# Two x1 pieces multiplied by g_final on VectorE instead of GpSimd, with the last wide block's end sums one step later

## The chip, the cores and the metric

One core of a Trainium2 chip runs the whole kernel; the other cores are idle. The metric is device time in microseconds (us) of one execution, the median over several runs. The core has TensorE (PE in the profile, with its weight loads as PEld), VectorE (DVE), ScalarE (ACT), GpSimd (POOL) and SyncE (SP); in this kernel SP computes nothing, it issues most of the DMAs.

## The reference

One encoder layer on 256 tokens of width 4096, in float32. What matters here is its end:

```python
x = x + einsum('bse,ed->bsd', concatenate([y_a, y_b]), w_out[i])       # x1 in the kernel
ple  = einsum('bsc,cd->bsd', p[i], w_ple[i])
gate = sigmoid(einsum('bsd,de->bse', rms_norm(x, g_ple[i]), w_ple_gate[i]))
x = x + ple * gate
return rms_norm(x, g_final)          # x * rsqrt(mean(x*x) + EPS) * g_final
```

The gate is a product of 256x4096 by 4096x4096. After it every row of x is squared and summed, and multiplied by the inverse root and by g_final, a gain for each of the 4096 columns.

## The kernel before

**Products.** A float32 product is made of three matmuls (`mm`, L130): each operand is split into a high half, rounded by ScalarE (`hi`, L115), and the rest, subtracted by VectorE (`lo`, L116). Rows 0-127 and 128-255 of the tokens are t=0 and t=1. A plain step takes one slice of 128 rows of a weight matrix and runs 12 matmuls of the block's column half-width for it.

**Blocks.** A `Block` (L772) makes 1024 columns of an output (the fourth block of the gate 768, so that its matmuls are 384 wide) from 32 weight slices. Some slices are taken in pairs by Strassen's scheme: `fast_steps` (L816) turns a pair into four steps, with four subtractions of weights (`sub`, L824) and the subtraction at L839 on VectorE besides the splits. `weave` (L155) lays the steps out; for the fourth block it is six pairs with plain steps between, then a trail. When the last step of the sixth pair has run, `wide_mid` (L1022) is spawned: it copies one bank and adds four others into `e` (L1027, L1029) and sets the flag `("mid", 3)`. When the last step of the block has run, `wide_done` (L1034) adds the last four banks, the **end sums** (L1049), in one step; in the next ones it takes the tanh of a quarter (L1053, ScalarE), multiplies it with the ple product (L1055), adds it to x1 (L1057, both VectorE) and squares the result with a row sum (L1060, ScalarE), quarter after quarter; at the end it reduces the sums of squares (L1064, L1065) and sets `part2`.

**Steps after the sixth pair.** In the order of TensorE they are called here c1, c2 (plain), e1, e2 (the ple product of the block, `wide_ple`), c3, c4 (plain), small (the ple product of the last 256 columns), c5, c6 (plain; c6 is the last of the block); then the last 256 columns of the gate in steps l0 to l7, of four weight slices each. l0 to l3 run for t=0 alone, l4 to l7 for both, and four more steps run t=1 with the kept halves of l0 to l3. The plain step inside the sixth pair, between its first and second step, is called cb. `done_last` (L1094) is spawned behind l7 for t=0 and behind the last step for t=1: tanh, product, sum, squares, then `finish` (L1108), which makes the inverse root and scales the eight 512-column pieces of x1 and sends them out. Pieces 1 and 4 (`EARLY`, L986) have been multiplied by g_final before and are scaled on ScalarE (L1123); the six others take both factors at once on VectorE (L1125).

**Order.** Every engine runs its instructions in the order in which the program emits them. The loop at L1452 does this for each step: load weights ahead (`fetch`), split the weights of a step some places ahead (`convert`), run the step's matmuls, then `advance()` (L240), which gives each spawned task one turn, up to its next `yield`, in the order in which they were spawned. A step with an `after` runs and advances before it converts. Four raw weight buffers (`raw`) and a ring of three split tiles (`hi`/`lo`) limit how far ahead loads and splits go: a raw buffer is free when VectorE has subtracted from it, a split tile when TensorE has used it.

**g_final.** `load_g` (L972) is spawned at the start of the fourth block. When the fourth pair has run (`z used`) it takes the two tiles `gF` and issues, one a step, eight DMAs on SP's queue (L979), each a piece of 512 gains broadcast to 128 partitions, in the order 1, 4, 0, 2, 3, 5, 6, 7. Behind the issue of piece 1 and of piece 4 it multiplies x1 by it on GpSimd, one instruction for each t (L983), four in all. SP's queue holds the weight loads of the same steps (L800, L998) between them.

Of the kernel before, what the change touches and what calls it, by code (L numbers as in the profile page):

```python
# [15 lines left out]
ALU = mybir.AluOpType  # L16
AX = mybir.AxisListType

P = 128
S = 256  # L20
NT = S // P
# [57 lines left out]
def encoder_layer(ctx: ExitStack, tc: tile.TileContext, x, p, positions, g_mix, w_in, g_q_latent, w_uq,  # L79
                  g_kv_latent, w_ukv, g_out_mla, g_out_dil, w_out, w_ple, g_ple, w_ple_gate, g_final,  # L80
                  c_inv, c_dist, out):
    nc = tc.nc
# [11 lines left out]
    def slot(tag, shape, dtype=F32):  # L94
        names[tag] = names.get(tag, 0) + 1
        return sp.tile([P, *shape], dtype, tag=tag, name=f"{tag}_{names[tag]}")
# [137 lines left out]
    flags, urgent, waiting, running = set(), [], [], []  # L234
# [469 lines left out]
    x1 = {}  # L704
# [239 lines left out]
    FAST, WIDE = 7, 4  # L944
# [27 lines left out]
    def load_g():  # L972
        while "z used" not in flags:
            yield
        for i in range(2):
            gF.append(slot(f"B{2 + i}", [2048]))
        for c in (1, 4, 0, 2, 3, 5, 6, 7):
            g = g_cols(512 * c)
            nc.sync.dma_start(g, g_final[512 * c:512 * (c + 1)].unsqueeze(0).to_broadcast([P, 512]))  # L979
            yield  # L980
            if c in EARLY:
                for t in range(NT):
                    nc.gpsimd.tensor_tensor(x1[c][:, t], x1[c][:, t], g, op=ALU.mult)  # L983

    P4 = {}
    EARLY = 1, 4  # L986
# [47 lines left out]
    def wide_done(k, blk):  # L1034

        def pieces(h, i):
            lo, out = 1024 * k + blk.q * h, []
            while lo < 1024 * k + blk.q * (h + 1):
                n = min(512 - lo % 512, 1024 * k + blk.q * (h + 1) - lo)
                at = lo - 1024 * k - blk.q * h  # L1040
                out.append((blk.e[:, i, at:at + n], x1[lo // 512], slice(lo % 512, lo % 512 + n), 2 * k + h + len(out)))
                lo += n
            return out

        def task():
            e, ps = blk.e, blk.ps
            quarters = ((0, 0, 0, "M2"), (3, 1, 1, "X"), (1, 0, 1, "M3"), (2, 1, 0, "M4"))
            for i, t, h, m in quarters:
                nc.vector.tensor_tensor(e[:, i], e[:, i], ps[m], op=ALU.add)  # L1049
            yield  # L1050
            for n in range(6):
                for i, t, h, m in quarters[n:n + 1]:
                    nc.scalar.activation(e[:, i], e[:, i], AF.Tanh, scale=r1h[:, t:t + 1])  # L1053
                for i, t, h, m in quarters[n - 1:n] if n else ():
                    nc.vector.scalar_tensor_tensor(e[:, i], e[:, i], 1.0, P4[t, h][:, :blk.q], op0=ALU.add, op1=ALU.mult)  # L1055
                    for u, xc, at, _ in pieces(h, i):
                        nc.vector.tensor_tensor(xc[:, t, at], u, xc[:, t, at], op=ALU.add)  # L1057
                for i, t, h, m in quarters[n - 2:n - 1] if n > 1 else ():
                    for u, xc, at, c in pieces(h, i):
                        nc.scalar.activation(u, xc[:, t, at], AF.Square, accum_out=ss2[:, t, c:c + 1])  # L1060
                yield
            if k == WIDE - 1:
                for t in range(NT):
                    nc.vector.tensor_reduce(part2[t], ss2[:, t, :9], axis=AX.X, op=ALU.add)  # L1064
                    nc.vector.tensor_scalar(part2[t], part2[t], 1.0 / DM, EPS, op0=ALU.mult, op1=ALU.add)  # L1065
                flags.add("part2")
        return task
# [23 lines left out]
    def g_cols(lo):  # L1091
        return gF[lo // 2048][:, lo % 2048:lo % 2048 + 512]
# [188 lines left out]
    for k in range(WIDE):  # L1281
        q = Q if k < 3 else 384
        order = weave(*((range(6), 6, 4), (range(7), 4, 4), (range(7), 4, 4), ((1, 2, 3, 4, 0, 5), 6, 6))[k], 2)
        blk = Block(w_ple_gate[:, 1024 * k:1024 * k + 2 * q], lhs_x1, x1_s, "x1_sums", order,
                    lambda kt: [("x1T", kt // 4)], LAST, "B6", WP + ["B4"], q)
        if k == 3:
            hook(len(steps), lambda: spawn(load_g()))
        lay(blk, order, wide_mid(k, blk), wide_done(k, blk), wide_ple(k, q), **({"after": [], "used": {4: "z used"}} if k == 3 else {}))
# [225 lines left out]
```

## Time and profile before

| what | value |
|---|---|
| median of 3 runs | 1931.02 us (1930.95 to 1931.32) |
| the profiled execution | 1929.53 us, of which the span is 1927.6 us |
| TensorE busy, weight loads | 1907.9 us (99%), 1630.7 us (85%) |
| VectorE busy | 1580.6 us (82%) |
| ScalarE busy | 1112.3 us (58%) |
| GpSimd busy | 81.2 us (4%), 126 instructions |
| granted TensorE clock | 0.998 of full speed |

Busy time of TensorE is modelled from pipelined matmuls, so that a busy TensorE is not always one at its peak; the distance between the starts of matmuls says more. The median and the profiled execution differ by 1.49 us. Span times below count from the first instruction of the profiled execution; some 1.9 us of its time lie outside the span.

### The profile page before, as it was taken

How to read it: one execution, taken by the hardware profiler on the slowest of the kernel's cores; microseconds unless marked ns; L12 is line 12 of the kernel's file. 1: busy time of each engine (PE TensorE's matmuls, PEld its weight loads, DVE VectorE, ACT ScalarE, POOL GpSimd, SP SyncE). 2: the span in 40 equal slices, each digit the busy share in tenths (PEclk: the TensorE clock that was granted, in tenths of full speed). 3: DMA queues.
4: the chain of work that ended last, by engine and by line, in shares of the span. 5: the costliest groups of instructions: out<-in, count | busy, mean ns of one | idle time of the engine just before them, and what ended most of it. 6: DMA issues, size and time to landing. Idle time of an engine off the chain costs nothing.

```text
span 1927.6 us, 25662 instructions
## 1 busy us (share of the span) xinstructions
PE 1907.9 (99%) x9254; PEld 1630.7 (85%) x9254; DVE 1580.6 (82%) x2198; ACT 1112.3 (58%) x1542; POOL 81.2 (4%) x126
## 2 busy tenths in 40 slices
PE   9999999999999999999999999999999999999997
PEld 8998889998888888888888888888888888888897
DVE  7767966665999999998877778889896698989896
ACT  6555565564655555655556666555564456656654
POOL 1001011220000000000000010000000000000010
PEclk9999999999999999999999999999999999999999
DMA  7666655555666666766665456665666656565675
GB/s 252 188 187 202 192 171 146 147 146 163 188 188 204 211 214 197 211 204 193 213 194 143 132 164 221 205 216 175 224 197 217 188 186 218 187 211 193 194 218 188
DMA packets 143119, 370.58 MB, mean 192 GB/s; under 512 B 12149, under 2 KB 41681, under 8 KB 142993
## 3 DMA queue, kind: packets, MB, share of 16 engines
q1 hardware_dynamic: 141360, 363.90, 61.8%
q0 software_dynamic: 1632, 5.05, 0.7%
q8 instruction: 72, 1.18, 0.3%
q14 instruction: 55, 0.44, 0.1%
HBM read 364.72 MB, written 4.19 MB: 191 GB/s over the span
## 4 chain that ended last, share of the span: by engine, by line
PE 90%; DVE 7%; DMA 1%; ACT 1%; issue 1%; SPq 0%; DVEq 0%; ACTq 0%
PE m L134 19%; PE m L135 19%; PE m L133 19%; PE t L133 4%; PE t L135 4%; PE t L134 3%; PE s L134 3%; PE s L133 3%; PE s L135 3%; PE o L134 3%; PE o L135 3%; PE o L133 3%; DVE lo L116 2%; DVE B L824 1%; DMA raw<-in_w_ple_gate_dram 1%
## 5 line engine op out<-in xcount | busy, mean ns | idle before, releaser
L116 DVE TENSOR_TENSOR lo<-raw,hi 128x1024 fp32r<-128x1024 f32 (+4 forms) x488 | 530.7, 1093 | 210.4 <-ACT hi L115 207.9
L115 ACT ACTIVATE hi<-raw 128x1024 fp32r<-128x1024 f32 (+4 forms) x488 | 463.1, 954 | 346.5 <-PE m L135 170.2
L133 PE MATMUL m<-hi,Ah 128*128 128x512 f32 (+3 forms) x1080 | 409.9, 380 | 0.1
L134 PE MATMUL m<-lo,Ah 128*128 128x512 f32 (+3 forms) x1080 | 405.7, 376 | 3.3 <-DVE lo L116 2.1
L135 PE MATMUL m<-hi,Al 128*128 128x512 f32 (+3 forms) x1078 | 403.0, 374 | 0.0
L134 PEld LDWEIGHTS m<-lo,Ah 128*128 128x128 f32 x1080 | 203.3, 188 | 35.7 <-DVE lo L116 7.2
L135 PEld LDWEIGHTS m<-hi,Al 128*128 128x128 f32 x1078 | 202.6, 188 | 30.4 <-DVE Al L127 0.2
L133 PEld LDWEIGHTS m<-hi,Ah 128*128 128x128 f32 x1080 | 203.3, 188 | 27.8 <-ACT Ah L125 0.3
L133 PE MATMUL m<-hi,B 128*128 128x512 f32 (+1 forms) x426 | 162.5, 382 | 0.0
L134 PE MATMUL m<-lo,B 128*128 128x512 f32 (+1 forms) x426 | 158.9, 373 | 0.2 <-DVE lo L116 0.2
L135 PE MATMUL m<-hi,B 128*128 128x512 f32 (+1 forms) x426 | 158.9, 373 | 0.0
L115 ACT ACTIVATE hi<-B 128x1024 fp32r<-128x1024 f32 (+1 forms) x85 | 87.9, 1035 | 92.3 <-DVE B L824 59.9
L116 DVE TENSOR_TENSOR lo<-B,hi 128x1024 fp32r<-128x1024 f32 (+1 forms) x85 | 101.0, 1190 | 5.0 <-ACT hi L115 2.1
L824 DVE TENSOR_TENSOR B<-raw,B 128x512 f32<-128x512 f32 (+1 forms) x138 | 94.9, 687 | 0.0
L135 PEld LDWEIGHTS m<-hi,B 128*128 128x128 f32 x426 | 80.0, 188 | 11.8
L134 PEld LDWEIGHTS m<-lo,B 128*128 128x128 f32 x426 | 80.2, 188 | 11.3 <-DVE lo L116 0.9
L133 PEld LDWEIGHTS m<-hi,B 128*128 128x128 f32 x426 | 80.1, 188 | 10.5
L115 ACT ACTIVATE B<-raw 128x1024 fp32r<-128x1024 f32 (+2 forms) x68 | 61.4, 910 | 47.7 <-DMA raw<-in_w_in_dram 20.0
L115 ACT ACTIVATE B<-B 128x1024 fp32r<-128x1024 f32 (+2 forms) x62 | 59.1, 954 | 43.3 <-DVE B L824 23.7
L116 DVE TENSOR_TENSOR B<-raw,B 128x1024 fp32r<-128x1024 f32 (+2 forms) x68 | 70.2, 1039 | 13.3 <-ACT B L115 13.0
L116 DVE TENSOR_TENSOR T<-t,T 128x512 fp32r<-128x512 f32 (+1 forms) x65 | 44.4, 682 | 41.6 <-ACT T L115 41.2
L839 DVE TENSOR_TENSOR lo<-raw,hi 128x1024 fp32r<-128x1024 f32 (+1 forms) x61 | 74.3, 1218 | 2.7 <-ACT hi L837 2.7
(764 smaller groups left out, 3879.3 us busy)
## 6 DMA issues: line engine op xcount, KB each, us to landing
raw<-in_w_in_dram SPq DMA_DIRECT2D x320, 512.0 KB, 3.9
raw<-in_w_out_dram SPq DMA_DIRECT2D x128, 512.0 KB, 4.4
raw<-in_w_ple_gate_dram SPq DMA_DIRECT2D x96, 512.0 KB, 4.6
raw<-in_w_in_dram SPq DMA_DIRECT2D x63, 400.0 KB, 3.5
raw<-in_w_uq_dram SPq DMA_DIRECT2D x32, 384.0 KB, 3.4
raw<-in_w_ple_gate_dram SPq DMA_DIRECT2D x32, 384.0 KB, 3.8
raw<-in_w_ukv_dram SPq DMA_DIRECT2D x16, 512.0 KB, 4.0
raw_l<-in_w_ple_gate_dram SPq DMA_DIRECT2D x8, 512.0 KB, 4.9
```

What stands on the lines that cost most here:

```text
L115: nc.scalar.activation(hi, src, AF.Copy)
L116: nc.vector.tensor_tensor(lo, src, plain(hi), op=ALU.subtract)
L133: nc.tensor.matmul(ps, ah, bh, start=start, stop=False)
L134: nc.tensor.matmul(ps, ah, bl, start=False, stop=False)
L135: nc.tensor.matmul(ps, al, bh, start=False, stop=stop)
L824: nc.vector.tensor_tensor(dst, a, b, op=ALU.subtract)
L839: nc.vector.tensor_tensor(lo, r[1], plain(hi), op=ALU.subtract)
```

## The change

`load_g` only issues the eight loads, one a step, in the same order. Then it waits for the flag that `wide_mid` of the fourth block sets, and in the two steps after the next one multiplies piece 1, then piece 4, of x1 by g_final, two instructions each, on VectorE. Nothing is computed on GpSimd there any more. In the fourth block `wide_done` gives away one turn before its end sums, so that these and all that follows in that task come one step later.

```diff
         for c in (1, 4, 0, 2, 3, 5, 6, 7):
-            g = g_cols(512 * c)
-            nc.sync.dma_start(g, g_final[512 * c:512 * (c + 1)].unsqueeze(0).to_broadcast([P, 512]))
-            yield
-            if c in EARLY:
-                for t in range(NT):
-                    nc.gpsimd.tensor_tensor(x1[c][:, t], x1[c][:, t], g, op=ALU.mult)
+            nc.sync.dma_start(g_cols(512 * c), g_final[512 * c:512 * (c + 1)].unsqueeze(0).to_broadcast([P, 512]))
+            yield
+        while ("mid", WIDE - 1) not in flags:
+            yield
+        for c in EARLY:
+            yield
+            for t in range(NT):
+                nc.vector.tensor_tensor(x1[c][:, t], x1[c][:, t], g_cols(512 * c), op=ALU.mult)
...
             e, ps = blk.e, blk.ps
             quarters = ((0, 0, 0, "M2"), (3, 1, 1, "X"), (1, 0, 1, "M3"), (2, 1, 0, "M4"))
+            if k == WIDE - 1:
+                yield
             for i, t, h, m in quarters:
                 nc.vector.tensor_tensor(e[:, i], e[:, i], ps[m], op=ALU.add)
             yield
```

## The prediction

> **What bounds the kernel.** I read the chain of waits first, then windows around the one place where GpSimd works late in the run, then each engine's timeline there.
>
> ```profile
> PE 90%; DVE 7%; DMA 1%; ACT 1%; issue 1%; SPq 0%; DVEq 0%; ACTq 0%
> ```
>
> TensorE bounds the run, so a change is worth what it gives or takes between two matmul starts, and behind the last matmul. Three windows of 10 us (span, then busy time and count of PE, PEld, DVE, ACT, POOL; clock, DMA share, GB/s):
>
> ```profile
> 1850.00:1860.00 10.00, 9.92 (x55) 9.38 (x55) 9.71 (x16) 5.87 (x9) 0.00 (x0) 1.00 0.74 212
> 1860.00:1870.00 10.00, 8.05 (x44) 7.09 (x42) 9.30 (x9) 2.55 (x4) 6.75 (x4) 1.00 0.96 317
> 1870.00:1880.00 10.00, 9.14 (x52) 9.06 (x53) 8.23 (x11) 5.88 (x8) 0.00 (x0) 1.00 0.72 210
> ```
>
> VectorE is busy all through the middle one but runs 9 instructions where 16 ran before. Its timeline (start, duration, engine, line, operation, form), then GpSimd's:
>
> ```profile
> 1856.13 0.55 DVE L824 TENSOR_TENSOR B<-raw,B 128x384 f32<-128x384 f32 x1
> 1856.60 0.95 DVE L839 TENSOR_TENSOR lo<-raw,hi 128x768 fp32r<-128x768 f32 x1
> ...
> 1862.95 1.92 DVE L116 TENSOR_TENSOR lo<-raw,hi 128x768 fp32r<-128x768 f32 x1 [0.70 <-ACT hi L115]
> 1864.80 1.63 DVE L824 TENSOR_TENSOR B<-raw,B 128x384 f32<-128x384 f32 x1
> 1866.35 2.03 DVE L839 TENSOR_TENSOR lo<-raw,hi 128x768 fp32r<-128x768 f32 x1
> 1868.30 1.64 DVE L824 TENSOR_TENSOR B<-raw,B 128x384 f32<-128x384 f32 x1
> 1869.86 0.94 DVE L116 TENSOR_TENSOR B<-B,B 128x768 fp32r<-128x768 f32 x1
> ```
>
> ```profile
> 1862.77 6.75 POOL L983 TENSOR_TENSOR T<-T,B 128x512 f32<-128x512 f32 x4 [406.28 <-DMA B<-in_g_final_dram]
> ```
>
> The same forms take 0.95 and 0.55 us before, two to three times that while L983 runs (until 1869.52), and 0.94 again right behind it. Starts of neighbours lie some 0.08 us closer than durations, so one 768-wide subtraction occupies VectorE for 0.87 us, a 384-wide one for 0.47. The four slow ones hold it from 1862.95 to 1869.86, 6.91 us; at the usual rate 2 x 0.87 + 2 x 0.47 = 2.68. TensorE pays (its waits of more than half a microsecond from 1850 on):
>
> ```profile
> 1864.93 0.44 PE L134 MATMUL m<-lo,Ah 128*128 128x384 f32 x1 [0.58 <-DVE lo L116]
> 1868.44 0.45 PE L134 MATMUL m<-lo,Ah 128*128 128x384 f32 x1 [1.13 <-DVE lo L839]
> 1870.86 0.44 PE L134 MATMUL m<-B,B7a 128*128 128x384 f32 x1 [1.11 <-DVE B L116]
> ...
> 1897.56 0.39 PE L134 MATMUL m<-lo,Ah 128*128 128x256 f32 x1 [0.54 <-DVE lo L116]
> ```
>
> **Removed: GpSimd's four multiplications.** Matmuls of 384 columns start every 0.173 us elsewhere. cb starts at 1864.01, and 30 matmuls follow until c1: without waits c1 starts at 1864.01 + 30 x 0.1733 = 1869.21, in the trace at 1872.92. That is 3.71 us; the three idle times shown make only 2.82, since a busy record is modelled longer than the spacing and each restart costs 0.11 more. VectorE's new times meet TensorE: cb's split done at 1863.9 (needed 1864.2), L839 at 1865.3 (1866.25), the third step's split at 1866.7 (1867.3), the fourth's at 1867.6 (1868.3). **Gain 3.71.**
>
> **What is late next: c1 and e1.** The loads of c1 and c2 were issued at 1860.87 and 1862.27, before the slowdown, and took 6.6 and 6.7 us behind the g_final pieces: landed 1867.47 and 1868.97. That stays. c1: ScalarE from 1867.57 (0.10 behind the landing, as cb's split shows at 1862.07), VectorE 0.88 later for 0.95, done at 1869.40; plus 0.06 from VectorE's end to the matmul (1864.87 to 1864.93). TensorE wants it at 1869.38: 0.08 of waiting and 0.11 for the restart. c2's split starts on VectorE at 1869.98 and occupies it to 1870.85; the four sums L1029 take 2.10 (1873.55 to 1875.65 in the trace), and e1's split is done at 1870.85 + 2.10 + 0.95 = 1873.90, wanted at 1869.21 + 0.19 + 24 x 0.1733 + 0.17 = 1873.73: 0.23 + 0.11. **Loss 0.19 + 0.34 = 0.53.** With everything earlier the second ple slice (issued at 1870.00 behind L824) and g piece 7 go out at about 1865.8. In the trace the transfers of this stretch land in order of issue, at 1865.80, 1866.47, 1867.47, 1868.04, 1868.97, 1869.65, 1870.60 and 1871.17, a 384 KB load about 1 us behind the one ahead, so I let later issues delay no earlier one.
>
> **Added: four multiplications on VectorE.** 128x512 in float32 from SBUF has a row, L824 in the earlier blocks: 683 ns, some 0.60 us of VectorE's time. Piece 1 stands behind e2's split and ahead of c3's, piece 4 ahead of c4's. e2's split ends its turn at 1874.70, so c3's comes at 1875.9, is done at 1876.9 and wanted at 1878.2; c4's is done at 1878.9, wanted at 1880.3. TensorE's trail, 2.08 us a plain step against 0.87 on VectorE, hides all 4 x 0.60 = 2.4 us; without that cover it would cost 2.4. One thing is late: c4's split frees the raw buffer for l0's load, 0.9 later than if all moved by 3.2. l0's load has that much to spare (landed at 1885.5, used at 1886.35), l1's next to none, should l0 push it; l1's split frees the buffer of l5's load. Between 0 and 0.9 I take **0.2**, since l1's load, issued 1.6 behind l0's, took only 0.6 longer (4.9 against 4.3).
>
> **Moved: the end sums.** VectorE around them (same columns):
>
> ```profile
> 1894.43 1.01 DVE L1049 TENSOR_TENSOR B<-B,m 128x384 f32<-128x384 f32 x2
> ...
> 1896.29 2.35 DVE L116 TENSOR_TENSOR lo<-raw_l,hi 128x1024 fp32r<-128x1024 f32 x2
> ...
> 1904.93 1.23 DVE L116 TENSOR_TENSOR lo<-raw_l,hi 128x1024 fp32r<-128x1024 f32 x1 [0.47 <-ACT hi L115]
> ...
> ...
> 1908.34 0.42 DVE L1102 SCALAR_TENSOR_TENSOR Q<-Q,t 128x256 f32<-128x256 f32 x1 [1.66 <-ACT Q L1101]
> ```
>
> Times of this trace, as if nothing had moved: 1.86 us of sums stand ahead of l4's split; TensorE waits for that (start spacings 0.82 and 0.23 for 0.12: 0.81 lost). Behind the change l4's and l5's splits come first (VectorE 1895.07 to 1897.64), then the sums to 1899.50, l6's split to 1900.64, three quarters (L1055, L1057: 3.32 us, as 1900.00 to 1903.32) to 1903.96, and l7's split, whose high half ScalarE makes behind the second quarter's squares at 1903.64: 1904.72 to 1905.95. l4 no longer waits, but l7 does: it starts 0.2 to 0.3 sooner, not 0.8. And the fourth quarter now lies behind l7's split: its sum done at 1907.0, its square at 1907.65, the four reductions at 1908.25; only then t=0's product, 1908.3 against 1908.34. From there VectorE works without a break to the last output. **Gain 0.05**; ends: 0.8 if l7's wait also goes, a loss of 0.5 if ScalarE's squares come later than this.
>
> **Sum:** -3.71 + 0.53 + 0.2 - 0.05 = -3.0 us: span 1924.6, that execution 1926.5. The profiled execution is 1.49 under the median; the same step from the median gives 1931.02 - 3.0 = **1928.0**.
>
> **Rivals.** (1) *More comes back*: c1 and e1 don't wait, and l4's stall goes through to the end: -3.71 - 0.8 = -4.5, 1926.5; with half of the 0.53 and of the 0.8, 1927.2. For it: the margins missed are 0.1 and 0.2 us. Against it: VectorE without a break at the end. (2) *Loads move past each other*: e1's, e2's and g piece 7, now issued up to 4 us earlier, share the queue with c1 and c2 instead of following them. 640 KB at 384 KB a microsecond are 1.67; c1 0.8 and c2 1.67 later make e1's split 1.7 later than above, TensorE loses 2.2 instead of 0.53, the gain is 1.3: 1929.7. Against it stand the eight landings in order. The Trainium skill speaks for it: the page "DMA: Bandwidth & Descriptors", section "Queues, rings and completion order", says that descriptors of a queue are consumed in ring order on each engine but that completion is not first in, first out; by that rule the sum would be -1.3, by the rows -3.0. (3) *Slower*: GpSimd is not the cause. VectorE is slow from 1862.95 because the g_final transfers fill the DMA engines (share 0.96), and stays so; then nothing is gained, 2.4 us are added to VectorE, of which the trail hides most, and l0's load is late: +0.4, 1931.4, and up to 1933.4 if the 2.4 are not hidden. It decides if L824 and L839 stay over 1.5 us around 1865. Against it: VectorE ran at its usual rate from 1859.9 to 1861.7, when the transfers were already queued, and again at 1869.86, 0.3 behind GpSimd's end.
>
> **Chances.** Forecast (gain 2.2 to 3.8) 0.55; (1) beyond 3.8: 0.22; (2) 0.15; (3) 0.05; others 0.03, half of them slower by much. What a measurement of this kernel tells from no change is taken as 0.2%, 3.86 us, and the forecast lies inside: faster by more 0.23, from (1); slower by more 0.04, from the exposed end of (3) and the others; within 0.73. Range: 1926.5 is the end of (1); 1930.3 takes in (2) with 0.6 more for l1's load; outside are (3), the others and the far tails of (1) and (2), under 2 in 10.
>
> **What would show it.** Right: L839 and both L824 of the last pair near 0.95 and 0.55 us; c1 at 1869.2 to 1869.5; waits of about 0.1 and 0.2 at c1 and e1; four multiplications of 0.68 us between e2's and c4's splits with no wait of TensorE behind them; no wait at l4 but one of about half a microsecond at l7. Wrong: slow VectorE without GpSimd, landings of c1 and c2 behind 1868 and 1869.5, a wait at c3 or c4, or t=0's tanh waiting long for the last square.

## The result, and the profile after

The changed kernel takes 1926.44 us (median of 9 runs, 1924.66 to 1928.93), the kernel before 1930.95 us beside it (9 runs, 1929.42 to 1931.51). The ratio is 0.9978, 95% interval 0.9968 to 0.9988; that is 4.2 us less, between 2.3 and 6.2. The profiled execution of the changed kernel took 1926.44 us as well.

From the page of the changed kernel: its span, the busy time of each engine, and the shares of the engines in the chain of work that ended last.

```profile
span 1924.7 us, 25658 instructions
...
PE 1906.5 (99%) x9254; PEld 1630.2 (85%) x9254; DVE 1579.3 (82%) x2202; ACT 1111.8 (58%) x1542; POOL 74.4 (4%) x122
...
PE 88%; DVE 7%; DMA 2%; ACT 1%; issue 1%; SPq 0%; DVEq 0%; ACTq 0%
```

The span is 2.9 us shorter than the 1927.6 of before. Four instructions have left GpSimd (126 to 122, 6.8 us), and VectorE's busy time fell by 1.3 us although it has four more: what it got is less than what it lost. TensorE still bounds the run.

The windows around the last pair of the changed kernel (bounds, length, then busy time and count of PE, PEld, DVE, ACT, POOL; clock, DMA share, GB/s):

```profile
1860.00:1868.00 8.00, 8.00 (x48) 8.00 (x48) 6.79 (x10) 3.88 (x6) 0.00 (x0) 1.00 1.01 316
1868.00:1871.00 3.00, 3.00 (x18) 2.82 (x17) 1.95 (x3) 1.89 (x4) 0.00 (x0) 1.00 1.06 410
1871.00:1875.00 4.00, 3.84 (x23) 3.52 (x22) 3.93 (x7) 2.21 (x3) 0.00 (x0) 1.00 0.70 249
```

And the same of the kernel before:

```profile
1860.00:1868.00 8.00, 6.73 (x38) 6.09 (x36) 7.30 (x7) 2.55 (x4) 5.23 (x4) 1.00 0.97 308
1868.00:1871.00 3.00, 1.46 (x7) 1.14 (x8) 2.88 (x4) 0.94 (x2) 1.52 (x1) 1.00 0.75 275
1871.00:1875.00 4.00, 4.00 (x23) 3.93 (x24) 3.97 (x6) 2.59 (x4) 0.00 (x0) 1.00 0.84 225
```

In the first eleven microseconds TensorE has 66 matmuls where it had 45, and VectorE does more instructions in less time. The DMA share is as high as before, so the transfers were not what slowed VectorE. The third window is where the changed kernel waits, for e1. VectorE's timeline of the changed kernel, from the sixth pair to t=0's product (start, duration, engine, line, operation, form):

```profile
1862.96 0.96 DVE L116 TENSOR_TENSOR lo<-raw,hi 128x768 fp32r<-128x768 f32 x1 [0.76 <-ACT hi L115]
1863.83 0.55 DVE L824 TENSOR_TENSOR B<-raw,B 128x384 f32<-128x384 f32 x1
1864.30 0.95 DVE L839 TENSOR_TENSOR lo<-raw,hi 128x768 fp32r<-128x768 f32 x1
1865.17 0.55 DVE L824 TENSOR_TENSOR B<-raw,B 128x384 f32<-128x384 f32 x1
...
1874.72 1.29 DVE L985 TENSOR_TENSOR T<-T,B 128x512 f32<-128x512 f32 x2
...
1876.80 1.29 DVE L985 TENSOR_TENSOR T<-T,B 128x512 f32<-128x512 f32 x2
...
1895.07 1.01 DVE L1053 TENSOR_TENSOR B<-B,m 128x384 f32<-128x384 f32 x2
...
1902.03 1.23 DVE L116 TENSOR_TENSOR lo<-raw_l,hi 128x1024 fp32r<-128x1024 f32 x1 [0.57 <-ACT hi L115]
...
1905.44 0.42 DVE L1106 SCALAR_TENSOR_TENSOR Q<-Q,t 128x256 f32<-128x256 f32 x1
```

L839 and both L824 are back at 0.95 and 0.55 us; the multiplications (now L985) take 1.29 a pair; the end sums (now L1053) lie behind l4's split; l7's split waits for ScalarE. t=0's product (now L1106) starts at 1905.44, 2.90 us sooner than before, and from it to the end both kernels take 19.26 us. TensorE's two long waits in this stretch of the changed kernel, at e1 and at l7:

```profile
1873.99 0.45 PE L134 MATMUL m<-lo,B 128*128 128x384 f32 x1 [0.16 <-DVE lo L116]
...
1903.31 0.39 PE L134 MATMUL m<-lo,Ah 128*128 128x256 f32 x1 [0.59 <-DVE lo L116]
```

### The profile page after: what moved, and what is told of

The parts are those of the page before. It is cut to its first block, busy times and chain, and to the rows that moved or that the text cites. A ratio compares the mean times of both kernels' runs of the same rounds, so it can differ in the third digit from the quotient of the medians.

```text
span 1924.7 us, 25658 instructions
## 1 busy us (share of the span) xinstructions
PE 1906.5 (99%) x9254; PEld 1630.2 (85%) x9254; DVE 1579.3 (82%) x2202; ACT 1111.8 (58%) x1542; POOL 74.4 (4%) x122
## 4 chain that ended last, share of the span: by engine, by line
PE 88%; DVE 7%; DMA 2%; ACT 1%; issue 1%; SPq 0%; DVEq 0%; ACTq 0%
PE m L134 19%; PE m L135 19%; PE m L133 19%; PE t L133 3%; PE t L134 3%; PE t L135 3%; PE s L134 3%; PE s L133 3%; PE s L135 3%; PE o L134 3%; PE o L135 3%; PE o L133 3%; DVE lo L116 2%; DVE B L824 1%; DVE B L116 1%
## 5 line engine op out<-in xcount | busy, mean ns | idle before, releaser
L824 DVE TENSOR_TENSOR B<-raw,B 128x512 f32<-128x512 f32 (+1 forms) x138 | 92.8, 672 | 0.0
L839 DVE TENSOR_TENSOR lo<-raw,hi 128x1024 fp32r<-128x1024 f32 (+1 forms) x61 | 73.2, 1200 | 1.8 <-ACT hi L837 1.7
```

Source lines behind the costliest of these rows:

```text
L824: nc.vector.tensor_tensor(dst, a, b, op=ALU.subtract)
L839: nc.vector.tensor_tensor(lo, r[1], plain(hi), op=ALU.subtract)
```

## The experiments

Medians of runs of one kernel scatter by more than the parts that are to be told apart. Below, the **stretch** is therefore used besides the ratio: in each profile, the time from VectorE's 768-wide split right ahead of the sixth pair's first two subtractions (L824) to the start of t=0's product. It leaves out what other parts of the run add by chance. It is 48.45 us before (1859.89 to 1908.34) and 45.60 after (1859.84 to 1905.44).

| kernel | median us (runs) | ratio to before [95%] | stretch us | from t=0's product to the end, us |
|---|---|---|---|---|
| changed | 1926.44 (9) | 0.9978 [0.9968, 0.9988] | 45.60 | 19.26 |
| mult_only | 1926.84 (11) | 0.9979 [0.9970, 0.9988] | 45.30 | 19.23 |
| sums_only | 1930.84 (11) | 0.9999 [0.9990, 1.0008] | 48.55 | 19.22 |
| no_mult | 1926.87 (11) | 0.9976 [0.9967, 0.9985] | 45.52 | 19.21 |
| gpsimd_trail | 1928.9 (11) | 0.9988 [0.9979, 0.9997] | 46.77 | 19.26 |
| vector_early | 1932.87 (11) | 1.0011 [1.0002, 1.0020] | see its section | 19.22 |
| g_late | 1929.35 (11) | 0.9990 [0.9981, 0.9999] | 44.38 | 22.38 |
| g_late_tail | 1928.53 (11) | 0.9989 [0.9980, 0.9998] | 44.49 | 22.20 |
| g_late_fixed | 1926.62 (11) | 0.9981 [0.9972, 0.9990] | 44.29 | 19.46 |

### Each half of the change alone

mult_only, against the changed kernel:

```diff
-            if k == WIDE - 1:
-                yield
             for i, t, h, m in quarters:
```

> Only the multiplications move to VectorE; the end sums stay where they were. Theory (GpSimd's reads slowed VectorE, and that is the whole gain): c1 starts at 1869.2 as in the changed kernel, e1 waits 0.3 to 0.4 us. In the tail the sums again stand ahead of l4's split, but l4's load lands late enough that they fit mostly before it: l4 waits some 0.3 more than in the changed kernel, l7 no longer waits, t=0's product starts about 1904.9 against 1905.44: span about 1924.2, gain over before 3.4. By the prediction as it stands (the moved sums gain 0.05) the span would be 1924.75. Rival (the later sums carry a part of the gain): span 1925.5 or more.

sums_only, against the kernel before:

```diff
+            if k == WIDE - 1:
+                yield
             for i, t, h, m in quarters:
```

> Only the end sums move one step; GpSimd multiplies as before. Theory: L839 and both L824 of the last pair stay at 1.6 to 2.0 us, c1 starts at 1872.9, l4's wait of 0.8 goes and l7 waits about 0.5 instead: span 1927.5, within 0.3 of before. Rival (the sums' place carries the gain): span 1926.8 or less.

mult_only has the whole gain. sums_only has none: 0.9999, and a stretch 0.10 us longer than before. Its TensorE still waits three times in the last pair (start to start 0.75, 1.47 and 1.45 us), and L839 is still slow. sums_only, VectorE's timeline:

```profile
1866.22 2.03 DVE L839 TENSOR_TENSOR lo<-raw,hi 128x768 fp32r<-128x768 f32 x1
```

The later end sums move a wait and do not remove it. l4 waits in mult_only, whose sums stand where they stood before; l7 waits in sums_only. TensorE of mult_only at l4, then of sums_only at l7:

```profile
1894.91 0.39 PE L134 MATMUL m<-lo,Ah 128*128 128x256 f32 x1 [0.48 <-DVE lo L116]
```

```profile
1906.36 0.39 PE L134 MATMUL m<-lo,Ah 128*128 128x256 f32 x1 [0.62 <-DVE lo L116]
```

From start to start it is 0.77 us in the one and 0.91 in the other, for 0.12 without a wait. mult_only's product for t=0 came at 1905.67, later than expected; 0.5 us of that is where its stretch began (1860.37, against 1859.84 in the changed kernel).

### Without the multiplications

no_mult leaves out the product of pieces 1 and 4 of x1 with g_final, for its time alone:

```diff
-        while ("mid", WIDE - 1) not in flags:
-            yield
-        for c in EARLY:
-            yield
-            for t in range(NT):
-                nc.vector.tensor_tensor(x1[c][:, t], x1[c][:, t], g_cols(512 * c), op=ALU.mult)
```

> The changed kernel without the four multiplications: pieces 1 and 4 of x1 are never multiplied by g_final. Theory: TensorE's trail hides VectorE's 2.4 us, so only what c4's late split costs can come back (l0's load 0.9 earlier, l4's up to 0.6): span 1924.1 to 1924.7 against 1924.7. Rival (VectorE is the bound and the multiplications are exposed): span 1922.3. If VectorE's slowness came from the g_final loads, which are all still there, L839 would be at 2 us here too.

Neither the ratio (0.9976) nor the stretch (45.52) is better than with them: the trail hides 2.4 us of VectorE's work. One reservation: in this execution c1's load landed late, its split came at 1869.67 and TensorE waited 0.66 us more there than in the changed kernel, while l7 waited 0.37 and not 0.87 from start to start. A TensorE that comes later to l7 waits less for it, so up to about half a microsecond of cost can't be excluded by this profile.

### GpSimd again, but where the trail runs

In gpsimd_trail the loads and the end sums are as in the change. VectorE's four multiplications are taken out, and the same four stand on GpSimd behind a small copy of the ple product (the copy only makes GpSimd wait until the step has run). The added lines:

```diff
+            if k == WIDE - 1:
+                nc.gpsimd.tensor_copy(acc[:, :64], P4[1, 1][:, :64])
+                for c in EARLY:
+                    for t in range(NT):
+                        nc.gpsimd.tensor_tensor(x1[c][:, t], x1[c][:, t], g_cols(512 * c), op=ALU.mult)
```

> The four multiplications stay on GpSimd but start behind ScalarE's last copy of the ple product (about 1879, a small GpSimd copy that reads it holds them back), in TensorE's trail. Theory if the place decides: GpSimd works from about 1879 to 1885, the splits of small, c5 and c6 take two to three times as long, TensorE has 1.3 us of room there and waits less than 0.5: span 1924.3 to 1925.2. Theory if GpSimd costs the same wherever it works: VectorE loses 4 us and TensorE about 3.7 as before: span 1927 to 1928.

It lies between: 0.9988, stretch 46.77, 1.2 us longer than the changed kernel and 1.7 shorter than before. GpSimd's timeline in gpsimd_trail, and then VectorE's:

```profile
1880.64 6.47 POOL L1019 TENSOR_TENSOR T<-T,B 128x512 f32<-128x512 f32 x4
```

```profile
1881.88 4.08 DVE L116 TENSOR_TENSOR lo<-raw,hi 128x768 fp32r<-128x768 f32 x2 [1.60 <-ACT hi L115]
1885.89 4.57 DVE L116 TENSOR_TENSOR B<-raw_l,B 128x1024 fp32r<-128x1024 f32 x3
```

Two 768-wide splits take 4.08 us (2.10 and 2.00 each) where two take 1.82 without GpSimd at work. One of the three 1024-wide ones takes 2.30 us, the other two 1.21. VectorE is as slow beside GpSimd here as it was in the last pair, with other operands, at another time, and the g_final loads long landed. The cost comes later: these splits free the raw buffers of the last steps, so that l4's load was issued at 1888.22 (1885.85 in the changed kernel), and TensorE of gpsimd_trail waits at l4 (and 0.69 us at l7):

```profile
1895.42 0.39 PE L134 MATMUL m<-lo,Ah 128*128 128x256 f32 x1 [0.87 <-DVE lo L116]
```

So the cause is GpSimd working beside VectorE, and where it does so sets how much of it TensorE pays.

### VectorE, but in the old place

vector_early is the kernel before with the later end sums and one word changed:

```diff
-                    nc.gpsimd.tensor_tensor(x1[c][:, t], x1[c][:, t], g, op=ALU.mult)
+                    nc.vector.tensor_tensor(x1[c][:, t], x1[c][:, t], g, op=ALU.mult)
```

> The four multiplications go to VectorE but stay at GpSimd's old place, each pair one step behind the issue of its g_final piece; the end sums one step later. Measured from the start of the sixth pair's first plain split to t=0's product (48.45 us in before, 45.60 in the changed kernel). Theory (the room in the trail counts, not the engine alone): VectorE now waits for the pieces to land (1862.6) with the pair's own subtractions queued behind, and adds 2.4 us where it is the bound: some 48, gain 0.5, span 1926.5 to 1928. Rival (VectorE is simply the right engine, wherever): 45.6 as in the changed kernel, span 1924.7.

It is slower than the kernel before, 1.0011 (1.0002 to 1.0020), and the expectation missed. VectorE's timeline of vector_early, then TensorE's:

```profile
1862.93 1.29 DVE L983 TENSOR_TENSOR T<-T,B 128x512 f32<-128x512 f32 x2 [3.61 <-DMA B<-in_g_final_dram]
1864.14 0.95 DVE L116 TENSOR_TENSOR lo<-B,hi 128x768 fp32r<-128x768 f32 x1
```

```profile
1865.15 0.69 PE L134 MATMUL t<-lo,B 128*128 128x384 f32 x1 [4.01 <-DVE lo L116]
1865.64 0.53 PE L135 MATMUL t<-hi,B 128*128 128x384 f32 x1
```

An engine runs its instructions in order. VectorE stood for 3.61 us in front of a multiplication whose gains had not landed; the split behind it, whose high half ScalarE had made by 1859.42, could have run; and TensorE was idle for 4.01 us. GpSimd in the same place waited for the same load and held up nobody while it waited. From 1864 to 1870 the granted clock was then 0.50, and the matmuls started every 0.32 us. From the 384-wide split at 1855.23 (1854.79 before, 1854.74 in the changed kernel) to t=0's product it is 55.95 us, against 53.55 before and 50.70 in the changed kernel. The other engine alone does not make the gain; the place behind the loads' landing is needed too.

### The profiled execution against the median

Before was 1.49 us under its median in its profile, and the change measured more than its profile shows. Three more profiles of before and one of the changed kernel ask where that lies.

> The kernel before once more, for a second profile of it. The first one was 1.5 us under the median of its runs, while the profiles of the changed kernel and of mult_only were at theirs. Theory: this stretch is stable (48.45 +- 0.2 us from the sixth pair's first plain split to t=0's product, the three waits 2.8 us again) and the executions differ ahead of it. Rival: the stretch itself is longer in an ordinary execution, 49.5 or more, so that the change gains more than the first profile shows.

> A third profile of the kernel before. In the second one TensorE's granted clock fell to about half from 1871.3 to 1874.6, behind the three waits that end in L134, and the stretch took 49.89 us (48.45 in the first). Theory: the drop belongs to the three waits and comes in some executions and not in others; the stretch is 48.4 to 48.6 without it or 49.7 to 50.2 with it, nothing between. Rival: the second profile was a disturbance of its own, and this one shows 48.5 again.

> A fourth profile, for the same question as the third: 48.4 to 48.6 us in the stretch with the clock at 1.00 throughout, or 49.7 to 50.2 with a drop behind the waits. If one more of the four drops, ordinary executions of before lose 0.4 to 0.8 us more on average than its first profile shows, and the change's gain in the median is larger than the 2.9 of the profiles by that much.

> The changed kernel once more. Theory: its longest wait before the last columns is 0.2 us of idle time, so that the clock stays at 1.00 there in every execution: 45.5 to 45.7 us in the stretch again. Rival (the drop comes from somewhere else than the waits): a drop between 1868 and 1880 here too, 46.5 or more.

The four stretches of before are 48.45, 49.89, 48.41 and 49.70 us; those of the changed kernel 45.60 and 45.02. So before_again went its rival's way (49.5 or more), the third and fourth profiles gave one of each of the two values expected, and the changed kernel stayed short. The two long ones have a lower clock. Windows of before_again (columns as above; the clock is the third number from the end):

```profile
1871.00:1872.00 1.00, 0.70 (x2) 0.70 (x3) 0.88 (x2) 1.00 (x3) 0.00 (x0) 0.60 0.76 127
1872.00:1873.00 1.00, 1.00 (x4) 1.00 (x4) 1.00 (x2) 1.00 (x3) 0.00 (x0) 0.50 0.84 274
1873.00:1874.00 1.00, 1.00 (x4) 1.00 (x4) 1.00 (x2) 0.18 (x1) 0.00 (x0) 0.50 0.80 250
1874.00:1875.00 1.00, 1.00 (x6) 1.00 (x6) 0.69 (x3) 0.00 (x0) 0.00 (x0) 0.70 0.80 162
```

TensorE of before_again behind the third wait:

```profile
1871.30 0.69 PE L134 MATMUL m<-B,B7a 128*128 128x384 f32 x1 [1.10 <-DVE B L116]
1871.79 0.52 PE L135 MATMUL m<-B,B7a 128*128 128x384 f32 x1
1872.11 0.52 PE L133 MATMUL t<-B,B7a 128*128 128x384 f32 x1
```

The starts are 0.32 us apart where 0.17 is usual, for some 3 us, and the stretch is 1.3 to 1.5 us longer. TensorE shows itself busy in all of it: only the clock column and the spacing tell. The three waits of the last pair stand in all four profiles; in two of them the clock falls at the third or right behind it. sums_only has the same three waits, and its clock stays at 1.00 from 1870 to 1875: with it, the clock fell in two of five executions. In the changed kernel's two profiles, and in those of mult_only and no_mult, those three waits are gone and the clock does not fall anywhere in the stretch.

The timed runs, each with its mean granted clock, point the same way. Over the three sets of runs of before, 23 of 75 had a mean of 0.996 or less, with a median of 1932.33 us against 1930.24 for the others; so had 4 of 11 of sums_only, but none of 9 of the changed kernel, none of 11 of mult_only and 1 of 11 of no_mult. A mean over the whole run does not say where the clock fell (in before_again it was also near 0.50 from 8 to 11 us), so this is no count of the falls in the stretch.

### Six g_final loads behind the weights

Two waits are left, at c1 and e1, whose loads stand behind the g_final pieces on SP's queue. Only pieces 1 and 4 are needed early. g_late, against mult_only:

```diff
-        for c in (1, 4, 0, 2, 3, 5, 6, 7):
+        def load(c):
             nc.sync.dma_start(g_cols(512 * c), g_final[512 * c:512 * (c + 1)].unsqueeze(0).to_broadcast([P, 512]))
+
+        for c in EARLY:
+            load(c)
             yield
...
+        while fetched[0] < len(steps):
+            yield
+        for c in (0, 2, 3, 5, 6, 7):
+            load(c)
+            yield
```

> mult_only with g_final's pieces 0, 2, 3, 5, 6, 7 loaded behind l7's weights instead of in the pairs; pieces 1 and 4 where they were. Theory (c1 and e1 wait because their loads queue behind those pieces): c1's load lands about 1.5 to 2 us sooner, c1 and e1 don't wait (0.53 us back), VectorE has l0's load out in time: 44.6 to 44.8 us in the stretch against 45.30 of mult_only, span about 1924.2 if what lies ahead takes as long as in mult_only. The late pieces land by 1900 and cost nothing. Rival (landings don't follow the order of issue, or the waits have another cause): 45.3.

g_late_tail is g_late with two splits moved ahead of other work of VectorE: l4's to before the end sums, and l7's to a turn earlier:

```diff
+        early = early and i != len(steps) - 13
...
+            if i == len(steps) - 8:
+                convert(lead + 1)
```

> g_late with two changes of order on VectorE: l4's split ahead of the end sums (which stay in their old step), and l7's split one turn earlier, ahead of the fourth quarter. Theory (the sums ahead of l4's split cost TensorE 0.77 in mult_only, and behind them l7's split was late): l4 and l7 both wait under 0.3, t=0's product comes 0.4 to 0.7 sooner than in g_late: 44.0 to 44.4 us in the stretch. Rival (VectorE without a break sets the tail whatever its order): as g_late.

g_late_fixed is g_late with the six loads two a step:

```diff
-            yield
+            if c in (2, 5):
+                yield
```

> g_late with its six late pieces loaded two a step, so that all are issued ahead of the first output. In g_late the sixth stood behind two outputs on SP's queue, which wait for t=0's scaling, and VectorE waited 2.75 us for it. Theory: that wait goes and nothing else changes: 44.4 us in the stretch, 19.3 to 19.6 from t=0's product to the end, some 0.9 us less than mult_only from the pair's first plain split to the end; ratio to before about 0.9974. Rival (the late loads collide with the outputs or with l7's weights in another way): as mult_only or slower.

In g_late both waits vanish and the stretch falls to 44.38, but the end grows from 19.2 to 22.38 us. SP's queue in g_late (L978 is the load of a piece, L1136 an output), then VectorE:

```profile
1909.51 0.82 SPq L1136 DMA_DIRECT2D out_dram<-T  x2
1910.38 0.45 SPq L978 DMA_DIRECT2D B<-in_g_final_dram  x1
1910.94 2.07 SPq L1136 DMA_DIRECT2D out_dram<-T  x4
```

```profile
1914.88 0.75 DVE L1135 SCALAR_TENSOR_TENSOR T<-T,st,B 128x512 f32<-128x512 f32 x1 [2.75 <-DMA B<-in_g_final_dram]
```

At one load a step the last one came onto the queue behind two outputs, at 1910.38, and VectorE waited 2.75 us for it. g_late_fixed mends that: stretch and end together are 63.75 us, against 64.53 for mult_only and 64.86 and 64.30 for the two profiles of the changed kernel. Its median (1926.62) shows no gain beside that of the change, though. In its profile the stretch began at 1861.75, 1.0 to 1.9 us later than in the other profiles without GpSimd in the last pair (vector_early aside), where the code is the same. One microsecond of it is a weight load of the pair before: issued at 1839.09 (1839.06 in g_late), it reached ScalarE at 1843.92 (1842.90 in g_late), and TensorE waited for the split behind it. ScalarE, then TensorE of g_late_fixed:

```profile
1843.92 0.85 ACT L115 ACTIVATE hi<-raw 128x768 fp32r<-128x768 f32 x1 [2.79 <-DMA raw<-in_w_ple_gate_dram]
```

```profile
1845.81 0.44 PE L134 MATMUL m<-lo,Ah 128*128 128x384 f32 x1 [0.46 <-DVE lo L116]
```

What made that load late is not shown, and one profile does not say how often it is; so whether the six later loads gain anything in the median stays open.

g_late_tail took l4's wait away and left 0.24 us at l7, with a stretch of 44.49: no gain over g_late, for t=0's product waits there for VectorE and ScalarE as well.

## Why the prediction came out as it did

**The bound, and the 3.71 us: right.** GpSimd's four multiplications were what stretched VectorE's; gpsimd_trail shows the slowdown again wherever the two overlap, and sums_only keeps it. c1 started at 1869.17 (forecast 1869.21).

**c1 and e1: right.** Loads of c1 and c2 reached ScalarE at 1867.48 and 1869.13 (forecast 1867.57 and 1869.07). c1's second matmul came 0.21 behind its first, e1's 0.50; with the restarts 0.14 and 0.44 us, 0.58 together for 0.53. g_late shows the reason: with the six pieces out of the way both waits are gone.

**Four multiplications hidden in the trail: right, as far as the runs can tell.** 0.68 us each, no wait at c3 or c4. The 0.2 us for l0's late load did not show: no matmul from l0 to l3 waited.

**The moved sums: direction at l4 and l7 right, size off.** The forecast was a gain of 0.05 us; sums_only has its stretch 0.10 longer. In the changed kernel l4 gained 0.60 us (0.81 forecast; its two starts of 0.23 and 0.22 still cost 0.21), and l7 lost 0.86 where 0.5 to 0.6 was forecast: ScalarE made l7's high half behind the second quarter's squares, as assumed, but at 1900.96, some 0.3 us later than the forecast's 1903.64 less the 2.98 by which everything moved. The bounds of -0.8 and +0.5 held.

**The sum for the profiled execution: right.** Span 1924.7 for 1924.6, a stretch 2.85 us shorter.

**From the profile to the median: mis-sized.** "The profiled execution is 1.49 under the median; the same step from the median gives 1931.02 - 3.0" took the step as the same in every execution. It is not: the profile used was one of the executions in which the clock stays up. In two of four the three waits came with some 3 us at 0.50, 1.3 to 1.5 us more; the changed kernel has no such waits, and its clock fell in neither of its two stretches. The mean stretch of before is 49.11 us over its four profiles, that of the changed kernel 45.31 over its two: 3.8 us, beside 4.2 measured between medians. The missing term is then about 0.7 us (half of 1.3 to 1.5). That the waits bring the fall is argued from its place and from where it is missing; no run changes the waits alone, and sums_only has them without it. What also remains open is how often the clock falls: so few profiles give only a rough share, and the interval of 2.3 to 6.2 us holds 3.0 as well.

The 4.2 us lie beyond the 2.2 to 3.8 that the forecast was given, where only rival (1) stood with its 0.22. The median, 1926.44, is at the very end of the range (1926.5; by the ratio it is 1926.8), and that end had been put there for rival (1), whose mechanism did not show. That the range reached so far is luck. The ratio's 0.22% lies on the 0.2% that was taken as the bound of "no change", and its interval (0.12 to 0.32%) holds that bound.

**Rivals.** (1) *More comes back* gave 1926.5 and the median is there, but its mechanism fell: c1 and e1 did wait, and l4's gain was lost again at l7. (2) *Loads move past each other* fell: the rows' answer held and c1's and c2's loads landed where the forecast had them, in order. The rule of the Trainium skill that spoke for it ("DMA: Bandwidth & Descriptors", "Queues, rings and completion order") was not seen at work here; one execution (no_mult) had c1's load land some 0.7 us later, measured from the start of its stretch, but in order too. (3) *GpSimd is not the cause* fell: the DMA share in the two windows of 1860 to 1871 is 1.01 and 1.06, and VectorE runs at its usual rate.

## What to carry to other kernels

An idle engine is not free help: before giving it side work, see in the trace whether the busy engine's same instructions get longer while it works, and what waits for those. Moving such work onto the in-order engine that feeds the bound paid here only behind the landing of what it reads, in a place where that engine had slack; in the old place, ahead of the landing, it cost more than the contention did. And one profile is one execution: when the median lies over a microsecond from it, profile the kernel again before carrying a sum from one to the other.

## What of the hardware was not expected

**A fixed price for each GpSimd instruction.** Beside GpSimd multiplications of 128x512 the slowed instructions of VectorE pay nearly the same amount whatever their own size: in before, 384-wide ones 1.63 for 0.55 us (+1.08), 768-wide ones 1.92 and 2.03 for 0.95 (+0.97, +1.08); in gpsimd_trail 1024-wide 2.30 for 1.21 (+1.09), 768-wide 2.10 and 2.00 (+1.15, +1.05). Four GpSimd instructions slowed four of VectorE's in the one, three in the other, where VectorE was idle until 1.24 us after the first began. So it reads as one instruction standing behind another, not as a shared rate. The Trainium skill says that ("SBUF — State Buffer", "Who interferes with whom": an exclusive lock, for a VectorE instruction with two inputs in SBUF against a GpSimd one that reads it), and the numbers agree.

**A clock that falls behind short waits.** In before the three waits are 0.5 to 1.1 us of idle time each, 2.8 in 7 us; in two of four executions the clock fell to 0.50 at the third or behind it, and in sums_only, with the same waits, it did not. In vector_early it fell behind one wait of 4.01 us, and was below full speed until about 1871. The Trainium skill ("TensorE: Matmul & The Clock Gate", "What's actually happening") has half rate after an idle window of about 3.4 us that runs freely, so that its effect varies from run to run. vector_early agrees with that and so does the variation; but no idle time of the last pair in the four profiles of before is over 1.16 us, so if the waits brought the fall, a window of partly idle time was enough, and how much idle time that takes is open.
